# Linear attention: the small tokens' norms cut at TensorE's waits, their steps dealt at half tiles and queued behind the newest projection matmul

## The chip, the cores and the metric

The kernel runs on one core of one Trainium2 chip. The metric is device time in microseconds (us); the median of three runs stands for a kernel. The profile is one further execution, recorded instruction by instruction. Engines are named as in the profile: PE is TensorE (matmuls), DVE VectorE, ACT ScalarE, POOL GpSimd, SP the engine that issues most DMAs.

## The reference, cut to what matters

One inference step of a decoder of two layers, for 1024 prompt tokens plus 16 meta tokens and for 8 single tokens of running sequences. The first layer is gated linear attention (GLA), the second differential attention over a paged cache; each is followed by a squared-ReLU MLP, and each of the four steps by a residual and a layer norm:

```python
x = layer_norm(ALPHA * x + gla(x), g, b)
x = layer_norm(ALPHA * x + (relu(x @ w1) ** 2) @ w2, g, b)
# the same with diff_attention in place of gla, in layer 1
```

The 8 sample tokens and the 16 meta tokens (24 of 32 columns) go through the same weights as the prompt. In the kernel they are the **small tokens**, and have a path of their own.

## The kernel before

All work is in fp32. A prompt matmul is split in three (`mm3`, L205 to L208): high part by high part, high by low, low by high. Weights are loaded as raw pieces (L191), split on ACT (`whi`, L193) and POOL (`wlo`, L194).

**The GLA phase** takes the first 500 us or so. Head by head (four heads), `proj(h)` (L369) projects q and k (four tiles of 512 columns, 24 matmuls each) and v (four tiles of two halves, 24 matmuls of 256 columns in each half). After each tile it yields. Then, twice per head, `decays` (L429) works out the decay factors and the masked scores on DVE, ACT and small matmuls (L452, L467, L487), and `advance` (L492) steps the state through four blocks (L500 to L504), which is a chain from PE to DVE and back. When the heads are done, four r units follow (L843 on): eight steps of two projection tiles, each with a Silu (L855) and transposes (L859). Then the output projection begins (`w_out`), and beside it the decode of the sample tokens with their paged keys (L911, L942, L943).

**The small tokens** are a generator, `small_tokens` (L779). In order it does: the GLA output projection (`s_rows`, L702, two weight steps), residual and norm (`s_post`, L725, and `s_ln`, L744), the first MLP's w1 in two halves (`s_cols`, L715, four steps each, a ReLU, a square, four transposes at L790), w2 (eight steps), residual and norm, and the second layer's projection (`wd`: four steps for q and k, with the rotation, and two for v, here called wv, with the stores of the new k and v rows). A weight step loads 2 MB into both buffers of the pool `swt`, and yields; at the next call come its 16 matmuls (L712 in `s_rows`, L723 in `s_cols`) and the loads of the step after it. A norm has four transposes (L734), and two small matmuls with a matrix of 1/1024 (L748, L754) that give mean and variance across partitions; between them DVE works, and behind them ACT's logarithm and exponential (L758, L759) and DVE again. All of this was one piece, written together with the last weight step before it.

**How it is dealt.** `deal` (L819) runs the generator to its next yield. It is called once ahead of the loop, after every second tile of `proj(1)` to `proj(3)` (four per head), after the decays (both halves in head 1, the second half in heads 2 and 3), and once in each of the eight r steps: 25 calls. The generator had 25 pieces.

**What sets the order.** The framework orders each engine's queue when the program is built. By a timing model of its own it gives an engine, at each moment, that one of its ready instructions that was written earliest. So an instruction may run far behind its place in the program, when its data are late, and later-written work runs ahead of it. Once built, each engine's order is fixed: if the data come later than the model thought, the engine stands. `tc.issue_after(x)` makes the instructions written in its block that run on x's engine come behind x in that order; it costs no wait on the chip. DMAs issued from SP are one such queue.

Of the kernel before, what the change touches and what calls it, by code (L numbers as in the profile page):

```python
# [21 lines left out]
P = 128  # L22
D = 1024
T = 1024
NB = 8
# [89 lines left out]
def hybrid_step(ctx, tc, A, dbg=None, upto=9):  # L115
# [89 lines left out]
    def mm3(ps, ah, al, bh, bl, first, last):  # L205
        TE.matmul(ps, ah, bh, start=first, stop=False)  # L206
        TE.matmul(ps, ah, bl, start=False, stop=False)  # L207
        return TE.matmul(ps, al, bh, start=False, stop=last)  # L208


    p1 = ExitStack()
# [131 lines left out]
    ps = smt()  # L343
# [16 lines left out]
    ps = smt()  # L360
# [9 lines left out]
    def proj(h):  # L370
        hi, lo = qku if h == 0 else qk_unit(h)
        hv, lv = (w.rearrange("p (i k n) -> p i k n", i=2, n=P) for w in (hi, lo))
        for c in range(h == 0, 2):
            cs = slice(512 * c, 512 * c + 512)
            for i in range(2):
                ps = mmt()
                for k in range(NB):
                    mm3(ps, hv[:, i, k, :], lv[:, i, k, :], XH[:, k, cs], XL[:, k, cs], k == 0, k == NB - 1)
                evict_qk(c, i, ps)
                yield  # L380
        hi, lo = v0u if h == 0 else kunit(wi, 1024 + h * 256)
        hv, lv = (w.rearrange("p (k n) -> p k n", n=256) for w in (hi, lo))
        for c in range(2):
            for i2 in range(2):
                ps = mmt()
                for i in range(2):
                    t = 4 * c + 2 * i2 + i
                    for k in range(NB):
                        a = slice(t * P, (t + 1) * P)
                        mm3(ps[:, i * 256 : (i + 1) * 256], XH[:, k, a], XL[:, k, a], hv[:, k, :], lv[:, k, :], k == 0, k == NB - 1)  # L390
                S.copy(Yh[:, h, 4 * c + 2 * i2 : 4 * c + 2 * i2 + 2, :].rearrange("p i e -> p (i e)"), ps)
                yield


    def rstd_of(ssum, n, scale, pool):
# [126 lines left out]
    first = proj(0)  # L522
    parts = []

    def early(c):
# [173 lines left out]
        TE.transpose(ps[:, m * P : (m + 1) * P], so[:, m * P : (m + 1) * P], ident)  # L699
    V.tensor_copy(soT.rearrange("p (h m) t -> p m h t", m=2), ps[:, :256].rearrange("p (m h t) -> p m h t", m=2, h=GH))  # L700

    def s_rows(lhs, w, nk):  # L702

        ps = smt()
        for k in range(0, nk, 4):
            ts = [sload2(w, k), sload2(w, k + 2)]
            yield
            for j in (1, 0):
                for i in range(2):
                    for c in range(2):  # L710
                        o = (2 * i + c) * TS
                        TE.matmul(ps[o : o + TS, :], lhs[:, k + 2 * j + i, :], ts[j][:, i, c * 512 : (c + 1) * 512], start=k == 0 and j == 1, stop=k == nk - 4 and j == 0)  # L712
        return ps

    def s_cols(lhs, w, c0):  # L715

        ps = smt()
        for k in range(0, NB, 2):
            ts = [sload(w[x * P : (x + 1) * P, c0 : c0 + 2048]) for x in (k, k + 1)]
            yield  # L720
            for j in (1, 0):
                for c in range(4):
                    TE.matmul(ps[c * TS : (c + 1) * TS, :], lhs[:, k + j, :], ts[j][:, c * 512 : (c + 1) * 512], start=k == 0 and j == 1, stop=k == NB - 2 and j == 0)  # L723
        return ps

    def s_post(ps, ln, pool):

        sev = ps
        if pool is spool:
            sev = s2()  # L730
            S.copy(sev, ps)
        pt = smt()
        for j in range(4):
            TE.transpose(pt[:, j * P : (j + 1) * P], sev[:, j * P : (j + 1) * P], ident)  # L734

        pv = pt.rearrange("p (j q c t) -> p q c j t", j=4, q=2, c=2)
        z = pool.tile([P, NB, TS], F32, name="sz")
        for c in range(2):
            zc = z[:, 4 * c : 4 * c + 4, :]
            V.scalar_tensor_tensor(zc, sx[:, 4 * c : 4 * c + 4, :], ALPHA, pv[:, 0, c], ALU.mult, ALU.add)  # L740
            V.tensor_tensor(zc, zc, pv[:, 1, c], op=ALU.add)
        s_ln(z, ln, pool)

    def s_ln(z, ln, pool):  # L744
        s1 = pool.tile([P, TS], F32, name="ss1")
        V.tensor_reduce(s1, z.rearrange("p k t -> p t k"), op=ALU.add, axis=AX.X)
        pm = smt()
        TE.matmul(pm[:, :TS], inv, s1, start=True, stop=True)  # L748
# [3 lines left out]
        V.tensor_reduce(s1, z2.rearrange("p k t -> p t k"), op=ALU.add, axis=AX.X)  # L752
        pm = smt()
        TE.matmul(pm[:, :TS], inv, s1, start=True, stop=True)  # L754
# [3 lines left out]
        S.activation(y, v, AF.Ln)  # L758
# [19 lines left out]

    def small_tokens():  # L779

        s_post((yield from s_rows(soT, A["gla_w_out"][0], NB)), 0, spool)
        shT = s4().rearrange("p (k t) -> p k t", t=TS)
        for half in range(2):
            ps = yield from s_cols(sx, A["mlp_w1"][0], half * 2048)
            r = s2()
            S.activation(r, ps, AF.Relu)
            V.tensor_tensor(r, r, r, op=ALU.mult)
            pt = smt()
# [4 lines left out]
        s_post((yield from s_rows(shT, A["mlp_w2"][0], 32)), 1, spool)  # L793

        pa = yield from s_cols(sx, wd, 0)
# [4 lines left out]
        pb = yield from s_rows(sx, wd[:, 2048:3072], NB)  # L800
        svv = s2()
        S.copy(svv[64:, :], pb[64:, :])
        S.copy(svv[:64, :], svv[64:, :])
        V.tensor_tensor(svv[:64, :], svv[:64, :], pb[:64, :], op=ALU.add)
        for c in range(2):
            hs = slice(4 * c, 4 * c + 4)
            o = 64 + c * TS
            f = lambda ap: ap.rearrange("t h d -> t (h d)")
            dma(f(A["k_rows_p"][0, 0, 0:NM, hs, :]), sqkr[o : o + NM, :])
            dma(f(A["k_rows_s"][0, :, 0, hs, :]), sqkr[o + NM : o + NM + NS, :])  # L810
            dma(f(A["v_rows_p"][0, 0, 0:NM, hs, :]), svv[c * TS : c * TS + NM, :])
# [30 lines left out]
    for h in range(GH):  # L842
# [3 lines left out]
        for c in range(2):  # L846
            cs = slice(512 * c, 512 * c + 512)
            sil, pts = [], []
            for m in range(2):
                ps = mmt()  # L850
                for k in range(NB):
                    ms = slice(m * P, (m + 1) * P)
                    mm3(ps, hv[:, k, ms], lv[:, k, ms], XH[:, k, cs], XL[:, k, cs], k == 0, k == NB - 1)
                s_ = silt[:, m, c, :]
                act = S.activation(s_, ps, AF.Silu).ins  # L855
                sil.append(s_)
# [658 lines left out]
    def samples():  # L1515

        sev = s2()
        dma(sev, A["srow"])
        s_post(sev, 2, hp)
        yield  # L1520

    stats = ln_stats(hp)
# [25 lines left out]
    def samples_out():  # L1548
# [7 lines left out]
        for u in range(2):  # L1556
# [7 lines left out]
        s_ln(z, 3, hp)  # L1564
        for u in range(2):
            ps = smt()
            for j in range(4):
# [210 lines left out]
```

## Time and profile before

| | us |
|---|---|
| runs shown | 2803.95, 2810.49, 2811.46 |
| median | 2810.49 |
| the profiled execution | 2806.01 |
| its span in the profile | 2804.1 |
| TensorE busy in the span | 2722.0 |
| VectorE busy in the span | 1956.1 |

The profiled execution is 1.9 us longer than its span. "Busy" of TensorE is modelled from the matmuls' sizes; where it stands still, the profile names what ended the wait. A row of waits reads: engine, tile and line that waited, what it waited for, us in total, how often, the longest. A row of the timeline reads: start, duration, engine, line, operation, output<-inputs, shape, count, and in brackets the idle time before it with its releaser. A row of windows has the stretch, its length, the busy time of PE, of PE's weight loads, of DVE, ACT and POOL (with instruction counts), then the granted TensorE clock as a share of full speed, the share of the DMA engines in use, and GB/s.

### The profile page before, as it was taken

The page shows a single profiled execution, that of the slowest core. Times are in us where ns is not written, and L with a number is a line of the kernel's source. Part 1 is how long each engine was busy: PE and PEld are TensorE (multiplying, and loading weights), DVE is VectorE, ACT ScalarE, POOL GpSimd, SP SyncE. Part 2 cuts the span into 40 slices and gives each one's busy share as a digit, 9 for nine tenths or more (in the row PEclk, how much of TensorE's full clock was granted, in tenths as well). Part 3 has the DMA queues.
Part 4 walks back from the last instruction along what each step waited for, and adds up shares of the span by engine and source line. Part 5 has one row for each costly group of instructions (what it writes and reads, how often), then busy time and mean ns, then how long its engine had stood idle before and what let it go on. Part 6 is the DMA issues. An engine that isn't in the chain of part 4 may idle for free.

```text
span 2804.1 us, 52239 instructions
## 1 busy us (share of the span) xinstructions
PE 2722.0 (97%) x19849; PEld 2235.8 (80%) x19849; DVE 1956.1 (70%) x3011; ACT 1107.8 (40%) x2266; POOL 1096.6 (39%) x744
## 2 busy tenths in 40 slices
PE   9989999999999999999999999899999999999997
PEld 6867767987777777777798988777899889798985
DVE  5375453678877777777568730887648888978788
ACT  4334463152231221222242112777525546355553
POOL 2132112234343443434234222100026677686774
PEclk9999999999999999999999999999999999999998
DMA  7475544735889898888658995212144555555684
GB/s 240 161 243 213 198 162 175 268 96 178 310 315 335 304 348 303 322 313 315 241 182 315 357 372 167 58 57 77 36 121 91 102 146 113 139 124 114 133 187 99
DMA packets 275624, 562.81 MB, mean 201 GB/s; under 512 B 23510, under 2 KB 144412, under 8 KB 271276
## 3 DMA queue, kind: packets, MB, share of 16 engines
q1 hardware_dynamic: 256076, 522.75, 54.1%
q0 software_dynamic: 19296, 36.71, 8.1%
q8 instruction: 156, 2.56, 0.4%
q14 instruction: 96, 0.79, 0.1%
HBM read 533.00 MB, written 29.52 MB: 201 GB/s over the span
## 4 chain that ended last, share of the span: by engine, by line
PE 81%; DVE 9%; ACT 4%; DMA 3%; issue 2%; POOL 1%; SPq 0%; DVEq 0%; POOLq 0%; ACTq 0%
PE mmt L206 19%; PE mmt L207 18%; PE mmt L208 18%; PE smt L983 4%; PE axt L206 3%; PE axt L207 3%; PE axt L208 3%; PE smt L1354 2%; ACT as L1332 1%; PE prt L1328 1%; DVE pg L942 1%; DMA swt<-in_mlp_w 1%; PE axt L1349 1%; DVE XH L203 1%; PE smt L723 1%
## 5 line engine op out<-in xcount | busy, mean ns | idle before, releaser
L194 POOL TENSOR_TENSOR wlo<-raw,whi 128x512 fp32r<-128x512 f32 x252 | 358.4, 1435 | 708.7 <-ACT whi L193 584.9
L206 PE MATMUL mmt<-whi,XH 128*128 128x256 f32 (+1 forms) x1760 | 523.5, 300 | 1.1 <-DVE ast L1330 0.9
L207 PE MATMUL mmt<-wlo,XH 128*128 128x256 f32 (+1 forms) x1760 | 521.6, 298 | 0.4 <-POOL wlo L194 0.4
L206 PE MATMUL mmt<-XH,whi 128*128 128x512 f32 (+1 forms) x1216 | 435.5, 359 | 6.4 <-DVE Y L1053 3.0
L208 PE MATMUL mmt<-XH,wlo 128*128 128x512 f32 (+1 forms) x1216 | 431.9, 356 | 0.0
L208 PE MATMUL mmt<-whi,XL 128*128 128x256 f32 x1536 | 431.6, 284 | 0.1
L193 ACT CAST whi<-raw 128x512 fp32r<-128x512 f32 x252 | 150.3, 619 | 575.0 <-PE mmt L208 193.0
L206 PEld LDWEIGHTS mmt<-whi,XH 128*128 128x128 f32 x1760 | 330.0, 188 | 39.9 <-issue 26.1
L943 DVE TENSOR_REDUCE sc<-pg 128x16 f32<-128x1024 f32 x256 | 308.3, 1211 | 67.5 <-POOL pg L942 65.0
L207 PEld LDWEIGHTS mmt<-wlo,XH 128*128 128x128 f32 x1760 | 331.7, 188 | 15.8 <-issue 5.5
L942 DVE TENSOR_TENSOR pg<-pg,qb 128x1024 f32<-128x1024 f32 x192 | 265.7, 1391 | 63.7 <-DMA pg<-in_cache_k 57.1
L207 PE MATMUL mmt<-XL,whi 128*128 128x512 f32 x768 | 306.9, 400 | 0.0
L208 PEld LDWEIGHTS mmt<-whi,XL 128*128 128x128 f32 x1536 | 287.8, 188 | 7.3 <-issue 6.8
L206 PEld LDWEIGHTS mmt<-XH,whi 128*128 128x128 f32 x1216 | 229.3, 189 | 50.3 <-issue 7.6
L942 POOL TENSOR_TENSOR pg<-pg,qb 128x1024 f32<-128x1024 f32 x64 | 165.5, 2587 | 257.1 <-DMA pg<-in_cache_k 139.9
L208 PEld LDWEIGHTS mmt<-XH,wlo 128*128 128x128 f32 x1216 | 229.4, 189 | 35.7 <-issue 2.9
L206 PE MATMUL mmt<-whi,HH 128*128 128x512 f32 x512 | 205.4, 402 | 5.2 <-DVE Y L1167 3.5
L208 PE MATMUL mmt<-whi,HL 128*128 128x512 f32 x512 | 204.5, 399 | 0.0
L207 PE MATMUL mmt<-wlo,HH 128*128 128x512 f32 x512 | 204.0, 398 | 0.0
L1617 POOL TENSOR_TENSOR wlo<-RW,whi 128x512 fp32r<-128x512 f32 x96 | 165.8, 1766 | 61.1 <-ACT whi L1616 57.2
L1617 POOL TENSOR_TENSOR wlo<-rw,whi 128x512 fp32r<-128x512 f32 x92 | 156.9, 1774 | 81.7 <-ACT whi L1616 78.5
L207 PEld LDWEIGHTS mmt<-XL,whi 128*128 128x128 f32 x768 | 145.4, 189 | 39.3 <-issue 8.0
(438 smaller groups left out, 5720.3 us busy)
## 6 DMA issues: line engine op xcount, KB each, us to landing
pg<-in_cache_k SPq DMA_DIRECT2D x256, 512.0 KB
pg<-in_cache_v SPq DMA_DIRECT2D x256, 512.0 KB
raw<-in_mlp_w SPq DMA_DIRECT2D x164, 256.0 KB
swt<-in_mlp_w SPq DMA_DIRECT2D x32, 1024.0 KB
rw<-in_mlp_w SPq DMA_DIRECT2D x116, 256.0 KB
RW<-in_mlp_w POOLq DMA_DIRECT2D x96, 256.0 KB, 5.7
swt<-in_gla_w_in SPq DMA_DIRECT2D x12, 1024.0 KB
swt<-in_diff_w_in SPq DMA_DIRECT2D x12, 1024.0 KB
```

The costliest lines, as they stand in the source:

```text
L193: S.copy(hi[:, c], raw)
L194: G.tensor_tensor(lo[:, c], raw, hi[:, c].bitcast(F32), op=ALU.subtract)
L203: return eng.tensor_tensor(lo, src, hi.bitcast(F32), op=ALU.subtract)
L206: TE.matmul(ps, ah, bh, start=first, stop=False)
L207: TE.matmul(ps, ah, bl, start=False, stop=False)
L208: return TE.matmul(ps, al, bh, start=False, stop=last)
L723: TE.matmul(ps[c * TS : (c + 1) * TS, :], lhs[:, k + j, :], ts[j][:, c * 512 : (c + 1) * 512], start=k == 0 and j == 1, stop=k == NB - 2 a ...
L942: eng.tensor_tensor(pg, pg, qb, op=ALU.mult)
L943: return V.tensor_reduce(sc[:, n, :], pg.rearrange("p (h d) -> p h d", d=64), op=ALU.add, axis=AX.X).ins
L983: m = TE.matmul(acc[i * TS : i * TS + 16, :256], w[r, n, :], pg[r, i * 256 : (i + 1) * 256], start=n == 0, stop=n == NPG).ins
L1354: TE.matmul(out, at, v, start=j == 0, stop=j == t + 1)
L1617: G.tensor_tensor(lo[:, k, :], t, hi[:, k, :].bitcast(F32), op=ALU.subtract)
```

## The change

1. **The norm is cut.** `s_post` yields after the copy that precedes its transposes (only in the GLA phase), `s_ln` before each of its two mean matmuls. The MLP's halves yield before their transposes. These yields give 1: the next step waits for another engine. The weight steps' yields give 0. The generator now has 33 pieces: three more for each of two norms, one more for each of two halves.
2. **First loads earlier.** The first loads of a weight matrix (`rows_in`, `cols_in`) are written before the norm or ReLU that precedes its matmuls, not behind it.
3. **Calls at half tiles.** `proj` also yields in the middle of each tile (0; after a whole tile it yields 1), and the r steps have three further calls: in the middle of both tiles, and after the first. These calls, and those after even tiles, run a piece only if the last piece ended with a 1. The 25 calls of before run always.
4. **Queued behind.** `mm3` notes its last matmul in `newest`, and `deal` runs the generator in `tc.issue_after(newest[0])`: a piece's matmuls come behind the projection matmul written last before them.
5. In the later phases, where `s_post` and `s_ln` are used again, their yields are run through at once.

```diff
     def mm3(ps, ah, al, bh, bl, first, last):
...
-        return TE.matmul(ps, al, bh, start=False, stop=last)
+        r = TE.matmul(ps, al, bh, start=False, stop=last)
+        newest[0] = r.ins
+        return r
...
                     mm3(ps, hv[:, i, k, :], lv[:, i, k, :], XH[:, k, cs], XL[:, k, cs], k == 0, k == NB - 1)
+                    if k == 3:
+                        yield 0
                 evict_qk(c, i, ps)
-                yield
+                yield 1
...
+                    if i == 0:
+                        yield 0
...
-    def s_rows(lhs, w, nk):
+    def s_rows(lhs, w, nk, ts):
         ps = smt()
         for k in range(0, nk, 4):
-            ts = [sload2(w, k), sload2(w, k + 2)]
-            yield
+            if k:
+                ts = rows_in(w, k)
+            yield 0
...
             S.copy(sev, ps)
+            yield 1
         pt = smt()
...
-        s_ln(z, ln, pool)
+        yield from s_ln(z, ln, pool)
...
         V.tensor_reduce(s1, z.rearrange("p k t -> p t k"), op=ALU.add, axis=AX.X)
+        yield 1
         pm = smt()
...
         V.tensor_reduce(s1, z2.rearrange("p k t -> p t k"), op=ALU.add, axis=AX.X)
+        yield 1
         pm = smt()
...
-    def deal():
-        next(small, None)
+    chain = [0]
+
+    def deal(any_=True):
+        if any_ or chain[0]:
+            with tc.issue_after(newest[0]):
+                chain[0] = next(small, 0)
...
-        for n, _ in enumerate(proj(h)):
+        n = 0
+        for whole in proj(h):
+            if not whole:
+                deal(False)
+                continue
             if n == 1:
                 state_out()
             next(updates, None)
-            if n % 2:
-                deal()
+            deal(n % 2)
+            n += 1
...
                     mm3(ps, hv[:, k, ms], lv[:, k, ms], XH[:, k, cs], XL[:, k, cs], k == 0, k == NB - 1)
+                    if k == 3:
+                        deal(False)
+                if not m:
+                    deal(False)
```

More of the change, by code (lines that the diff above doesn't have):

```diff
@@ L520, in head_end @@
         G.tensor_tensor(Yh[:, h], Yh[:, h], bc(rr, [P, 8, 256], 2), op=ALU.mult)
-    first = proj(0)
+    first = (x for x in proj(0) if x)
     parts = []
@@ L713, in s_rows, with s_cols @@
         return ps
[L715 removed]
+    def s_cols(lhs, w, c0, ts):
         ps = smt()
         for k in range(0, NB, 2):
[L719 to L720 removed]
+            if k:
+                ts = cols_in(w, c0, k)
+            yield 0
             for j in (1, 0):
@@ L779, in small_tokens @@
     def small_tokens():
-        s_post((yield from s_rows(soT, A["gla_w_out"][0], NB)), 0, spool)
+        w1, w2 = A["mlp_w1"][0], A["mlp_w2"][0]
+        wo = A["gla_w_out"][0]
+        ps = yield from s_rows(soT, wo, NB, rows_in(wo, 0))
+        ts = cols_in(w1, 0, 0)
+        yield from s_post(ps, 0, spool)
         shT = s4().rearrange("p (k t) -> p k t", t=TS)
         for half in range(2):
-            ps = yield from s_cols(sx, A["mlp_w1"][0], half * 2048)
+            ps = yield from s_cols(sx, w1, half * 2048, ts)
+            ts = rows_in(w2, 0) if half else cols_in(w1, 2048, 0)
             r = s2()
@@ L792, in small_tokens @@
                           pt.rearrange("p (j c t) -> p c j t", j=4, c=4))
-        s_post((yield from s_rows(shT, A["mlp_w2"][0], 32)), 1, spool)
-        pa = yield from s_cols(sx, wd, 0)
+        ps = yield from s_rows(shT, w2, 32, ts)
+        ts = cols_in(wd, 0, 0)
+        yield from s_post(ps, 1, spool)
+        pa = yield from s_cols(sx, wd, 0, ts)
+        wv = wd[:, 2048:3072]
+        ts = rows_in(wv, 0)
         sqkr = s2()
@@ L1518, in samples @@
         dma(sev, A["srow"])
-        s_post(sev, 2, hp)
+        for _ in s_post(sev, 2, hp):
+            pass
         yield
@@ L1563, in samples_out @@
             V.scalar_tensor_tensor(zc, sx[:, 4 * u : 4 * u + 4, :], ALPHA, zc, ALU.mult, ALU.add)
-        s_ln(z, 3, hp)
+        for _ in s_ln(z, 3, hp):
+            pass
         for u in range(2):
```

10 lines of the change are left out of this document (8 added, 2 removed).

## The prediction, as put on record

> **What bounds the kernel now.** I read the page first, then the waits of TensorE over the stretch in which the small tokens' work is dealt out (150 to 515 us), then that stretch's timeline.
>
> ```profile
> span 2804.1 us, 52239 instructions
> PE 2722.0 (97%) x19849; PEld 2235.8 (80%) x19849; DVE 1956.1 (70%) x3011; ACT 1107.8 (40%) x2266; POOL 1096.6 (39%) x744
> ```
>
> ```profile
> PE smt L748 <- DVE ss L746: 3.5, 1, 3.5
> PE smt L723 <- DMA swt<-in_mlp_w: 2.7, 2, 2.2
> PE axt L452 <- DVE gAd L461: 2.7, 2, 1.6
> PE smt L712 <- DMA swt<-in_mlp_w: 2.2, 1, 2.2
> PE axt L501 <- DVE gS L504: 2.1, 2, 1.5
> PE smt L712 <- DMA swt<-in_gla_w_out: 1.3, 1, 1.3
> PE axt L500 <- ACT At L475: 1.2, 1, 1.2
> ```
>
> TensorE is the bound. It is busy in 97% of the span, so a wait matters only where TensorE itself stands. In these 365 us the rows add up to 15.7 us of standing still; those of the small tokens (L748, L723, L712) are 9.7 us. After the longest, TensorE also ran slowly:
>
> ```profile
> 185.00:190.00 5.00, 1.54 (x33) 1.30 (x28) 4.93 (x11) 0.42 (x2) 2.77 (x2) 0.74 0.98 325
> 190.00:195.00 5.00, 5.00 (x14) 3.91 (x15) 5.00 (x12) 2.03 (x6) 0.46 (x1) 0.57 0.59 172
> 235.00:240.00 5.00, 5.00 (x78) 3.74 (x71) 0.60 (x2) 1.77 (x5) 0.00 (x0) 0.66 0.71 234
> ```
>
> ```profile
> 166.83 0.59 ACT L391 COPY Y<-mmt 128x512 f32<-128x512 f32 x1 [5.09 <-PE mmt L208]
> ```
>
> ```profile
> 177.95 0.60 PE L734 MATMUL smt<-c_ident,s 128*128 128x128 f32 x4
> 189.01 0.64 PE L748 MATMUL smt<-ss,c_inv 128*128 128x32 f32 x2 [3.46 <-DVE ss L746]
> 189.83 0.80 PE L206 MATMUL mmt<-XH,whi 128*128 128x512 f32 x1
> 194.26 0.40 PE L207 MATMUL mmt<-XL,whi 128*128 128x512 f32 x1
> 195.20 0.40 PE L208 MATMUL mmt<-XH,wlo 128*128 128x512 f32 x1
> 210.45 1.92 PE L723 MATMUL smt<-swt,sx 128*32 128x512 f32 x16
> 234.14 2.64 PE L723 MATMUL smt<-swt,sx 128*32 128x512 f32 x16 [2.20 <-DMA swt<-in_mlp_w]
> ```
>
> The granted clock (third figure from the end) was 0.57 from 190 to 195. Ten projection matmuls took 4.43 us (189.83 to 194.26), where four took 0.94 us just after (194.26 to 195.20), that is 2.35 us for ten: 2.1 us lost on top of the 3.46. The piece at 234.14 took 2.64 us where the one at 210.45 took 1.92.
>
> **The first norm and the first half of the MLP: nothing, 0 us.** Each piece is now to be queued behind the newest projection matmul written before it, and the norm is cut at its waits. The order edge binds only where a piece stands ahead of that matmul in TensorE's order. It does not here. The first norm's steps are dealt between the halves of head 1's v tiles. The last of those tiles was evicted at 166.83, while the norm's transposes stand at 177.95, its first mean matmul at 189.01, the next weight pair at 210.45. They run late because they wait for the decode state and for 2 MB of weights per piece, not because of where they are written. So every edge is already met, and among ready instructions all of these still rank ahead of head 2's work. L748 was put where the builder's own timing expected the sum of L746, and VectorE came 3.46 us later than that. The change alters neither, so I leave this wait and its slow spell in place. Bounds: if a shifted priority removes it, -5.6 us; if an order moves against it, +2 us, the size of the other waits.
>
> **One call lost.** Before, 25 pieces met 25 calls. After, there are 33 pieces, and 25 calls that always run; the others run only when the last piece ended at a wait. All such extra steps find a conditional call next, except one: the second half of the first MLP ends its ReLU in the last call of head 2's projections, and the next call is the whole one inside head 2's second decay. It is spent on four transposes. From there each weight pair comes one whole call later, and the last pair (wv, second four rows) is left for the loop behind the r projections. Where that moves something:
>
> ```profile
> 339.12 1.06 PE L712 MATMUL smt<-swt,s 128*32 128x512 f32 x8
> 347.36 0.50 PE L206 MATMUL mmt<-XH,whi 128*128 128x512 f32 x1
> 389.59 1.92 PE L712 MATMUL smt<-swt,s 128*32 128x512 f32 x16
> 407.49 0.41 PE L754 MATMUL smt<-ss,c_inv 128*128 128x32 f32 x2
> 411.06 0.70 PE L500 MATMUL axt<-Y,At 128*128 128x256 f32 x2 [1.20 <-ACT At L475]
> 416.45 1.92 PE L723 MATMUL smt<-swt,sx 128*32 128x512 f32 x16
> 418.30 0.70 PE L501 MATMUL axt<-gS,t 128*128 128x256 f32 x2
> 431.51 1.92 PE L723 MATMUL smt<-swt,sx 128*32 128x512 f32 x16
> 488.19 1.92 PE L712 MATMUL smt<-swt,sx 128*32 128x512 f32 x16
> ```
>
> ```profile
> 408.38 1.28 ACT L758 ACT_TABLE_LOAD   x1
> 409.81 1.20 ACT L475 COPY At<-gAd 32x128 f32<-32x128 f32 x4
> 423.76 1.58 ACT L855 ACTIVATE st<-mmt 128x512 f32<-128x512 f32 x3
> ```
>
> Up to 339 the later call is still met. The fourth pair of w2 (339.12) may now only follow head 3's last v tile, so about 347; those behind it follow at the pace of the loads, 12 us apiece (210.45 to 234.14 are two), and the eighth (389.59) goes to about 400, behind the second r unit's first two tiles. TensorE has projection tiles for all of that time: 0 us. Its norm then moves too: L754 may come only in the tile that starts after the Silu at 423.76, so about 427.
>
> This takes work out of the one place of the stretch where TensorE has nothing else: until 424 the chain of head 3's last decay and state steps sets the time. Three things leave it: the table load and logarithm ahead of the At copies, worth the 1.20 us that TensorE waits at 411.06; the pair at 416.45, after which L501 starts at 418.30 (1.85 us); L754's 0.41. One thing enters: the eighth w2 pair, up to 1.92 us, of which I take 1. Sum -2.4 us, bounds -3.5 and +1.
>
> A page has another price here. The Trainium skill (ScalarE: Activation LUTs, "What ACT_TABLE_LOAD costs") gives about 2.66 us for each change of table, 1.28 of load and 1.38 of drain; by it the gain would be 1.4 us larger. This trace shows no drain: the load at 408.38 lasts 1.28 us and the copies start at 409.81, one 0.23 us activation later.
>
> **The tail.** From 431.51 to 488.19 five pairs stand behind five r units. Five still do, but the last pair follows them, in the output projection. The pair that used the idle place at 416 now lies where TensorE is full: +1.9 us. Its weights can only be asked for when the pair at 488 is done. Waits for swt were 0.5 to 2.2 us in this trace; I take 1.5, bounds 0 and 3 (2.20 and the 0.72 us that 234.14 was slow).
>
> ```profile
> 495.80 1.97 SPq L811 DMA_DIRECT2D out_v_rows_p<-s  x1
> 499.41 2.65 SPq L191 DMA_DIRECT2D raw<-in_gla_w_out  x2
> 505.89 4.13 SPq L911 DMA_DIRECT2D pg<-in_cache_k  x4
> ```
>
> ```profile
> 508.65 0.62 ACT L193 CAST whi<-raw 128x512 fp32r<-128x512 f32 x1 [13.23 <-DMA raw<-in_gla_w_out]
> ```
>
> ```profile
> 600.00:650.00 50.00, 47.62 (x213) 37.90 (x213) 37.37 (x40) 19.90 (x36) 17.18 (x10) 1.00 0.39 117
> 650.00:700.00 50.00, 49.09 (x210) 39.02 (x209) 45.49 (x44) 9.79 (x17) 19.14 (x10) 1.00 0.61 196
> 700.00:750.00 50.00, 47.67 (x278) 35.59 (x277) 38.33 (x43) 13.83 (x25) 18.71 (x11) 1.00 0.78 277
> ```
>
> Behind it come the stores of v rows (495.80), and in the same SP queue raw weights and the first key pages. These may come 10 to 15 us later. The pages are dealt as background work, which TensorE's own matmuls cover; a late start costs only where VectorE is tight, 600 to 750, where TensorE stands 5.6 us in all: 0 taken, bounds -3 and +3.
>
> **Sum.** 0 + 0 - 2.4 + 1.9 + 1.5 + 0 = +1.0 us. The profiled execution took 2806.0 us, so 2807.0 on its scale. The runs shown are 2803.95, 2810.49 and 2811.46, and with the profiled one their mean is 2808.0; its median lies 4.5 above the profile. On that middle I forecast 2809. About 0.3%, 8.4 us from the median, is what a measurement of this kernel can tell from no change.
>
> **Rivals.**
> *The waits go.* If the builder's new order puts the small pieces later than their data, L748's 3.46 and 2.1 go, and the swt waits (1.3, 2.7, 2.2) with two slow spells of about 0.7: 5.6 + 6.2 + 1.4 = 13.2. The rest of the sum stays: 2808.0 + 1.0 - 13.2 = 2796. For it: 9.7 us of small-token waits exist and nothing else need use them. Against: no edge binds before 339. Chance 0.27. The Trainium skill (TensorE: Matmul & The Clock Gate, Part 1) lets the clock halve after an idle window of about 3.4 us; by it the 2.2 us gaps would cost nothing more, and this rival would give 1.4 us less. The trace disagrees: 0.66 was granted from 235 to 240, after a gap of 2.20.
>
> *Slower: the last pair blocks SP's queue.* SP issues in order. If the stores of the last pair stand ahead of the raw weights of the second output unit and come 10 to 12 us late, the cast at 508.65 (which already waited 13.23 us for such a raw) comes at about 520, past the 513 or so at which TensorE has used the first unit on both halves of the tokens (estimated: from 490.1, 192 matmuls of 256 columns at half the 0.235 us of one of 512). That is 7 us, a slow spell of 2, and the 3 us wait of the pair itself: 12 us, 2820. It decides from a delay of about 5 us on. For it: the two raws at 499.41 do stand behind those stores now. Against: the order is made anew, and the raws then come first if they are ready first. Chance 0.20.
>
> **Numbers.** Forecast 0.53 (own range 2803 to 2819: all its bounds, without the -5.6 that is the first rival's), waits go 0.27, SP blocked 0.20. Range 2793 to 2820, reaching into both rivals. Faster by over 0.3% 0.27, same 0.53, slower 0.20.
>
> **What would show it.** Right: L748 still waits about 3 us near 189; the w2 pairs keep their places before 339, then lie 8 us or more later; no Ln between head 3's At copies; a pair of wv after 490. Wrong: L748 and the swt rows gone from TensorE's waits (first rival), or new waits of L206 on whi or wlo between 505 and 530 (second). A change of over 5 us that arises after 750 would mean that I missed a place altogether.

## The result, and the profile after

The changed kernel takes 2819.31 us (median of 20 runs, 2811.05 to 2838.1), the kernel before in the same session 2809.28 (20 runs, 2799.43 to 2815.79): a ratio of 1.0037 with an interval of 1.0026 to 1.0048, so 10 us slower. Its profiled execution took 2819.02 us (before 2806.0).

```profile
span 2817.1 us, 52238 instructions
PE 2724.5 (97%) x19849; PEld 2236.5 (79%) x19849; DVE 1957.5 (69%) x3011; ACT 1109.5 (39%) x2267; POOL 1089.9 (39%) x744
```

The engines are as busy as before (TensorE 2724.5 against 2722.0), so the 13 us of span are not work. The waits of TensorE from 150 to 530 us, in the same view that the prediction began with:

```profile
PE smt L768 <- DVE ss L765: 3.6, 1, 3.6
PE axt L460 <- DVE gAd L469: 2.6, 2, 1.6
PE axt L460 <- issue: 2.5, 1, 2.5
PE smt L729 <- DMA swt<-in_gla_w_out: 2.1, 1, 2.1
PE axt L508 <- ACT At L483: 1.8, 1, 1.8
PE smt L741 <- DMA swt<-in_mlp_w: 1.7, 2, 1.3
PE smt L729 <- DMA swt<-in_mlp_w: 1.1, 1, 1.1
```

Lines are shifted by the diff: L748 is now L768, L712 L729, L723 L741, L452 L460. The longest wait stays (3.6 us, before 3.5), and so do those for weights: 2.1, 1.7 and 1.1 us, against 1.3, 2.7 and 2.2. What is new here is 2.5 us at L460 that no releaser explains.

To see where the time went I use three marks that each trace has: the first matmul of the output projection (call it P), the projection matmul near 706 us that waits 1.25 us for HL in every kernel (M), and the end of the span. Two rows of before and two of after, from the timeline of TensorE:

```profile
490.05 0.38 PE L206 MATMUL mmt<-whi,XH 128*128 128x256 f32 x1
706.03 0.50 PE L206 MATMUL mmt<-XH,whi 128*128 128x512 f32 x1 [1.25 <-DVE HL L203]
```

```profile
486.57 0.39 PE L206 MATMUL mmt<-whi,XH 128*128 128x256 f32 x1
708.95 0.50 PE L206 MATMUL mmt<-XH,whi 128*128 128x512 f32 x1 [1.24 <-DVE HL L203]
```

P comes 3.5 us earlier than before; from P to M it takes 222.4 us instead of 216.0, so 6.4 more; from M to the end 2108.2 instead of 2098.1. The table in the next section shows that only the middle one of these three differences lasts from profile to profile.

Most of that difference arises in the output projection itself. Its end is marked by the first matmul of 512 columns behind it, before and after:

```profile
584.05 0.48 PE L206 MATMUL mmt<-XH,whi 128*128 128x512 f32 x1
```

```profile
585.27 0.39 PE L206 MATMUL mmt<-XH,whi 128*128 128x512 f32 x1
```

From P to here it takes 94.0 us before and 98.7 after, so 4.7 more; from here to M 122.0 and 123.7, so 1.7 more.

Inside P to M, the last pair and the waits that are new with it (timeline of TensorE of the changed kernel):

```profile
484.71 1.92 PE L729 MATMUL smt<-swt,sx 128*32 128x512 f32 x16
496.33 1.92 PE L729 MATMUL smt<-swt,sx 128*32 128x512 f32 x16
537.40 0.50 PE L206 MATMUL mmt<-whi,XH 128*128 128x256 f32 x2 [0.96 <-ACT whi L193]
538.78 0.38 PE L207 MATMUL mmt<-wlo,XH 128*128 128x256 f32 x1 [0.17 <-POOL wlo L194]
540.66 0.39 PE L207 MATMUL mmt<-wlo,XH 128*128 128x256 f32 x1 [0.20 <-POOL wlo L194]
554.01 0.38 PE L207 MATMUL mmt<-wlo,XH 128*128 128x256 f32 x1 [0.37 <-POOL wlo L194]
642.27 0.50 PE L206 MATMUL mmt<-whi,HH 128*128 128x512 f32 x1 [2.24 <-DVE Y L1208]
657.80 0.50 PE L206 MATMUL mmt<-whi,HH 128*128 128x512 f32 x1 [1.22 <-DVE Y L1208]
661.80 0.50 PE L206 MATMUL mmt<-whi,HH 128*128 128x512 f32 x1 [0.92 <-DVE Y L1208]
```

The next to last pair is at 484.71. The last, whose 2 MB go into the same two buffers, follows at 496.33, within the output projection, without a wait of its own. Then TensorE waits four times for converted weights and three times for VectorE. Before, these are all its waits from 500 to 698, and none is for weights:

```profile
628.01 0.50 PE L206 MATMUL mmt<-XH,whi 128*128 128x512 f32 x1 [0.68 <-DVE HL L203]
641.36 0.50 PE L206 MATMUL mmt<-whi,HH 128*128 128x512 f32 x1 [1.70 <-DVE HL L203]
658.87 0.51 PE L206 MATMUL mmt<-whi,HH 128*128 128x512 f32 x1 [0.38 <-DVE Y L1167]
```

What SP and ScalarE did about 530, first before, then after:

```profile
529.35 0.90 SPq L191 DMA_DIRECT2D raw<-in_gla_w_out  x2
```

```profile
533.13 0.62 ACT L193 CAST whi<-raw 128x512 fp32r<-128x512 f32 x1 [7.55 <-DMA raw<-in_gla_w_out]
534.22 0.62 ACT L193 CAST whi<-raw 128x512 fp32r<-128x512 f32 x1 [0.47 <-DMA raw<-in_gla_w_out]
```

```profile
509.48 0.33 SPq L841 DMA_DIRECT2D out_v_rows_p<-s  x1
513.70 0.36 SPq L952 DMA_DIRECT2D pg<-in_cache_k  x1
515.82 13.87 SPq L952 DMA_DIRECT2D pg<-in_cache_k  x12
529.79 0.39 SPq L191 DMA_DIRECT2D raw<-in_gla_w_out  x1
531.44 0.39 SPq L191 DMA_DIRECT2D raw<-in_gla_w_out  x1
```

```profile
536.73 0.62 ACT L193 CAST whi<-raw 128x512 fp32r<-128x512 f32 x1 [12.57 <-DMA raw<-in_gla_w_out]
538.62 0.62 ACT L193 CAST whi<-raw 128x512 fp32r<-128x512 f32 x1 [1.27 <-DMA raw<-in_gla_w_out]
```

The first page is asked for 27.1 us behind P (513.70 - 486.57), before 15.8. Twelve more follow in one row up to 529.7, and behind them the third unit's raw weights: asked for at 529.79 and 531.44 (43.2 and 44.9 us behind P; before, 39.3 and 39.8), cast 6.9 and 7.2 us later (before, the first 3.8). As many pages stand ahead of them in SP's queue as before (13 and 14; before 14), so it is not a changed place in that queue that makes them late. VectorE, which multiplies the pages, has less to do meanwhile. The window from 490 to 520 of before, then of after (busy time of DVE is the third busy time):

```profile
490.00:520.00 30.00, 30.00 (x257) 29.95 (x254) 14.95 (x26) 4.40 (x8) 5.87 (x4) 1.00 0.99 344
```

```profile
490.00:520.00 30.00, 30.00 (x255) 28.42 (x254) 9.69 (x23) 2.65 (x5) 2.57 (x2) 1.00 0.91 286
```

The DMA engines move less as well, 286 GB/s instead of 344. From 20 to 30 us behind P, where SP's queue stands at the stores of the v rows, their share is 0.64; before it is 1.03 (a packet counts where it starts, so a share can pass 1).

### The profile page after: what moved, and what is told of

It reads as the page before. It is cut to its first block, busy times and chain, and to the rows that moved or that the text cites. A ratio compares the mean times of both kernels' runs of the same rounds, so it can differ in the third digit from the quotient of the medians.

```text
span 2817.1 us, 52238 instructions
## 1 busy us (share of the span) xinstructions
PE 2724.5 (97%) x19849; PEld 2236.5 (79%) x19849; DVE 1957.5 (69%) x3011; ACT 1109.5 (39%) x2267; POOL 1089.9 (39%) x744
## 4 chain that ended last, share of the span: by engine, by line
PE 75%; DVE 11%; DMA 5%; ACT 4%; issue 3%; POOL 2%; SPq 1%; DVEq 0%; POOLq 0%; ACTq 0%
PE mmt L206 17%; PE mmt L207 17%; PE mmt L208 17%; PE smt L1024 4%; PE axt L206 3%; PE axt L207 3%; PE axt L208 3%; PE smt L1395 2%; ACT as L1373 1%; DVE pg L983 1%; DVE XH L203 1%; DVE Y L1733 1%; DVE RX L1634 1%; PE prt L1369 1%; DMA swt<-in_mlp_w 1%
## 5 line engine op out<-in xcount | busy, mean ns | idle before, releaser
L206 PEld LDWEIGHTS mmt<-XH,whi 128*128 128x128 f32 x1216 | 229.5, 189 | 49.4 <-issue 8.4
```

## Experiments

My theory after the first profile: the lost call puts the last pair behind P, and pages and weights of the output projection come late by it. The rivals: the cuts, the half tiles or the queueing cost by themselves; or the loss lies behind M (+10 us in the first profile), where the orders of the engines differ in a few places only.

All runs in one table. "Page" is the first page's issue less P; "output projection" runs from P to the first matmul of 512 columns behind it. The last column is the ratio to the kernel before, timed on the same chip, with its interval.

| kernel | P | page | output projection | P to M | M to end | ratio |
|---|---|---|---|---|---|---|
| before | 490.1 | 15.8 | 94.0 | 216.0 | 2098.1 | |
| d_queue_only | 486.7 | 15.9 | 93.9 | 214.5 | 2104.0 | 0.9996 (0.9982 to 1.0010) |
| h_no_relu_cut | 491.7 | 17.8 | 93.9 | 215.8 | 2103.7 | 0.9983 (0.9970 to 0.9995) |
| changed | 486.6 | 27.1 | 98.7 | 222.4 | 2108.2 | 1.0037 (1.0026 to 1.0048) |
| a_again | 490.0 | 27.0 | 99.4 | 220.7 | 2104.7 | 1.0038 (1.0024 to 1.0052) |
| e_no_queue | 490.2 | 26.8 | 99.0 | 222.4 | 2094.4 | 1.0042 (1.0027 to 1.0057) |
| c_one_call_less | 489.4 | 27.1 | 99.0 | 220.9 | 2099.0 | 1.0024 (1.0010 to 1.0038) |
| b_call_back | 497.9 | 16.3 | 95.0 | 217.7 | 2102.7 | 1.0008 (0.9994 to 1.0022) |
| i_two_calls_less | 487.9 | 40.4 | 102.4 | 235.0 | 2101.7 | 1.0035 (1.0017 to 1.0053) |
| j_pages_held | 488.2 | 28.4 | 93.5 | 223.8 | 2104.9 | 1.0025 (1.0013 to 1.0036) |
| g_v_rows_queue | 490.0 | 25.6 | 99.2 | 221.3 | 2095.1 | 1.0018 (1.0004 to 1.0032) |
| k_y_late | 491.6 | 20.4 | 99.4 | 220.8 | 2099.7 | 1.0015 (0.9997 to 1.0033) |
| l_before_y_late | 490.9 | 12.6 | 95.8 | 219.4 | 2099.6 | 1.0021 (1.0007 to 1.0036) |
| n_last_unloaded | 485.3 | 16.3 | 94.5 | 216.7 | 2100.9 | 1.0005 (0.9992 to 1.0017) |
| q_1mb_more | 493.2 | 18.5 | 94.8 | 217.4 | 2104.3 | 1.0018 (1.0003 to 1.0032) |
| m_2mb_more | 492.0 | 20.6 | 100.0 | 231.9 | 2101.9 | 1.0061 (1.0039 to 1.0082) |

The first three have one and the same order on every engine, so their spread is that of the measurement: 5 us in P, 0.1 in the output projection, 1.5 in P to M, 6 in M to end, and 0.17% in the ratio. The interval of h_no_relu_cut misses 1 although its order is that of before. So a ratio within 0.2% of 1 shows nothing here by itself, even where its interval misses 1.

**a_again**: the changed kernel, unchanged.

> The changed kernel once more, unchanged, for a second profile. Lost call (my step: the last wv pair falls behind the r units): ratio 1.003 to 1.005, and the places where it lies behind the kernel before are the same as in the first profile: +3 to +4 us by 700. Chance in the late stretches: the jumps at 1910, 2333 and 2450 (about +9 us together in the first profile, where the order on every engine is that of the kernel before) are gone or elsewhere. A cause that lasts: they are there again.

P to M is 220.7, and the output projection takes 99.4; from M to the end it takes 2104.7, about what d_queue_only and h_no_relu_cut take. The 10 us behind M in the first profile were scatter, and the rival that puts the loss there falls.

**d_queue_only**: the kernel before with point 4 of the change alone.

```diff
...
-        next(small, None)
+        with tc.issue_after(newest[0]):
+            next(small, None)
```

> The kernel before with its pieces queued behind the newest projection matmul, and neither the cut norm nor the half tiles. My step that no edge binds: ratio 0.999 to 1.001, and the profile of the kernel before, a measure also of how much two profiles of one order differ in the late stretches. If the edges bind: a ratio beyond 0.3% either way.

0.9996, and every engine's order is that of before. Queueing alone does nothing.

**c_one_call_less**: the kernel before with one deal fewer.

```diff
-            if c or h == 1:
+            if h == 1 or (c and h == 3):
                 deal()
```

> The kernel before with one deal fewer (none at head 2's second decay), nothing else of the change: its last pieces slip by one call as they do in the changed kernel. Lost call: ratio 1.002 to 1.005 over the kernel before. The cut norm, the half tiles or the queueing: 0.999 to 1.001.

1.0024, and P to M is 220.9, the output projection 99.0, like those of the changed kernel. A lost call alone brings the loss in P to M.

**b_call_back**: the changed kernel with the call given back.

```diff
             with tc.issue_after(newest[0]):
                 chain[0] = next(small, 0)
+                if any_ and chain[0]:
+                    chain[0] = next(small, 0)
```

> The change with its lost call given back: a call that always runs and finds a step of the chain pending runs that step and the next piece, so that the last wv pair stands inside the r units again. Lost call: the loss goes, ratio 0.998 to 1.001, and the waits of L206 and L207 on whi and wlo between 537 and 554 are gone. The cut norm, the half tiles or the queueing themselves: ratio stays at 1.003 to 1.004.

1.0008, not told from 1; page as before, output projection 95.0, and P to M 2.3 above the mean of the first three rows. One wait for wlo of 0.8 us is left at 558, so that part of the expectation did not hold fully. Its profile lost 8 us ahead of P, 3 of them before 100 us.

**h_no_relu_cut**: the changed kernel without one line.

```diff
             V.tensor_tensor(r, r, r, op=ALU.mult)
-            yield 1
             pt = smt()
```

> The changed kernel without its one yield behind the ReLU of the first MLP's halves; all other cuts, the half tiles and the queueing stay. Its instructions then stand in the order of the kernel before on every engine. Lost call: ratio 0.999 to 1.001, and the output projection takes 94 us from its first matmul to the first of 512 columns behind it, as before. If the other cuts cost something by themselves: a ratio above 1.001.

0.9983. With the yield behind the ReLU gone, the order of all five engines is the order before: the cut norms, the earlier first loads, the half tiles and the queueing together move no instruction. Without this one yield the change has no effect, neither gain nor loss.

**e_no_queue**: the changed kernel without the queueing.

```diff
-            with tc.issue_after(newest[0]):
-                chain[0] = next(small, 0)
+            chain[0] = next(small, 0)
```

> The changed kernel without the queueing behind the newest projection matmul; the cuts, the half tiles and the lost call stay. Crowded DMA behind the lost call: nothing comes back, ratio 1.002 to 1.004, first page about 27 us behind the start of the output projection, waits for whi and wlo of 1.5 to 2.5 us. If the queueing, harmless in the kernel before, costs together with the cuts: ratio 0.999 to 1.001.

1.0042, pages at 26.8, output projection 99.0, six waits for whi and wlo of 1.8 us in all: nothing comes back. The queueing takes no part in the loss. It does in what the change wins ahead of P: from the Exp behind head 3's last decays to P it takes 83.0 us here, 81.4 in both profiles of the changed kernel, and 83.7 in all three of the order before. Here the second norm's second small matmul (L775) stands at 411.93, within that stretch; in the changed kernel it comes at 424.10.

**i_two_calls_less**: two deals fewer.

```diff
-            if c or h == 1:
+            if h == 1:
                 deal()
```

> The kernel before with two deals fewer (none at the second decay of heads 2 and 3): two wv pairs lie in the output projection. Lost call: twice the cost or more in the output projection, 94 us become 103 to 105, ratio 1.004 to 1.008. If one lost call costs by its place in head 2's decay and not by the tail: about as with one deal fewer, 1.002 to 1.003.

Two pairs lie behind P, the pages come 40.4 us behind it, and P to M takes 235.0, 19.6 more than the mean of the first three rows (215.4), 8.5 of them in the output projection. That is more than twice the 5.4 of one call. The ratio, 1.0035, is lower than that would give (about 1.007); its interval reaches to 1.0053.

**j_pages_held**: the kernel before, its pages held by their page table; no pair is moved and no more bytes. Two page steps are dealt at once when the table is let go.

```diff
-    dma(ptab, A["page_table"])
...
-                if side and (n == 4 if scaled else n < 12):
+                if side and not scaled and n == 2:
+                    with tc.issue_after(steps_v[-1]):
+                        V.memset(ptab, 0)
+                    dma(ptab, A["page_table"])
+                    for _ in range(2):
+                        next(side)
+                if side and (n == 4 if scaled else 1 < n < 12):
                     next(side)
```

> The kernel before with the page table, and so the first page, held until the third tile of the output projection is evicted (about 10 us later); all pairs stay where they are. Late pages: waits for whi and wlo of 1 to 3 us appear in the output projection, which takes 95.5 to 97 us instead of 94, ratio 1.0005 to 1.0015. The pair itself: 94 us, ratio 0.999 to 1.0005.

The ratio is 1.0025, more than I expected, and the loss is at another place: the output projection takes 93.5 us (before 94.0, the changed kernel 98.7), but TensorE then waits for VectorE, and from there to M it takes 130.2 us instead of 122.0. The rows of TensorE, then those of VectorE ahead of 633:

```profile
606.06 0.50 PE L206 MATMUL mmt<-XH,whi 128*128 128x512 f32 x1 [2.63 <-DVE HL L203]
633.37 0.79 PE L206 MATMUL mmt<-XH,whi 128*128 128x512 f32 x1 [3.87 <-DVE HL L203]
711.97 0.50 PE L206 MATMUL mmt<-XH,whi 128*128 128x512 f32 x1 [1.25 <-DVE HL L203]
```

```profile
626.88 2.31 DVE L941 TENSOR_TENSOR pg<-pg,qb 128x1024 f32<-128x1024 f32 x1
629.23 1.22 DVE L942 TENSOR_REDUCE sc<-pg 128x16 f32<-128x1024 f32 x1
630.37 2.35 DVE L1128 SCALAR_TENSOR_TENSOR Y<-Y,ht 128x1024 f32<-128x1024 f32 x2
632.63 1.28 DVE L203 TENSOR_TENSOR HL<-mmt,HH 128x512 fp32r<-128x512 f32 x2
```

So a late start of the pages costs by itself, nearly 9 us over the mean of the first three rows behind the output projection. VectorE was busy 10.84 us from 490 to 520 here and 14.95 before. 100 us later a page's product and sum (626.88 and 629.23) stand in its order ahead of the HL that TensorE waits for at 633.37.

**g_v_rows_queue**: the last pair's four stores issued by ScalarE.

```diff
...
-            dma(f(A["v_rows_p"][0, 0, 0:NM, hs, :]), svv[c * TS : c * TS + NM, :])
+            nc.scalar.dma_start(f(A["v_rows_p"][0, 0, 0:NM, hs, :]), svv[c * TS : c * TS + NM, :])
...
```

> The changed kernel with the four stores of the v rows issued from ScalarE's queue instead of SyncE's; nothing else moves by more than a place. Late pages (the last pair's stores hold SyncE's queue, the first pages come 8 us later and fill the DMA engines when the third unit's raw weights are asked for): the first page comes 2 to 8 us earlier, the waits for whi and wlo between 535 and 557 (1.7 to 2.5 us) go, the output projection takes 96 to 97 us instead of 98.7 to 99.5, ratio 1.002 to 1.003. The pair itself and its weights: 98.7 to 99.5 as in the changed kernel, waits stay, ratio 1.0035 to 1.004.

Inconclusive. The pages came at 25.6 instead of 27, the output projection takes 99.2 and P to M 221.3: the stores alone were not what held SP. The ratio, 1.0018, is below the changed kernel's 1.0037, but the two intervals overlap. In the changed kernel the first store waited 4.6 us for the loads of the residual x (Y) ahead of it; here the next load in the queue waited 3.5 us for raw weights in its place.

**k_y_late** and **l_before_y_late**: in the changed kernel and in the kernel before, two of the four 1 MB loads of Y are held until tiles 3 and 5 of the output projection.

```diff
+                if not scaled and n in (2, 4):
+                    u2 = 2 + (n == 4)
+                    with tc.issue_after(steps_v[-1]):
+                        V.memset(Yt[:, 0, u2 * 256 : u2 * 256 + 1], 0.0)
+                    y_in(u2)
...
```

> The changed kernel, its lost call kept, with the loads of the last two quarters of the residual x (Y, 1 MB each) held until tiles 3 and 5 of the output projection are evicted, so that they no longer stand ahead of the pages in SyncE's queue. Late pages: the first page comes 5 us earlier or more (22 us behind the start of the output projection instead of 27), VectorE is busier between 490 and 520 than the 8.6 to 9.7 us of the changed kernel, the stretch from 480 to 700 loses 1 to 4 us less than in the changed kernel (+4.6 to +7.4), ratio 1.001 to 1.003. The pair itself: stretch and ratio as in the changed kernel, 1.0035 to 1.004.

> The kernel before with the same two loads held. If each us by which the pages come earlier is worth half a us, as the held pages cost about half a us for each us later: first page 10 to 13 us behind the start of the output projection instead of 15.8, ratio 0.998 to 0.9995. If before was at the point where the pages are early enough: 0.9995 to 1.0005.

In the first the pages come at 20.4 instead of 27, but the output projection still takes 99.4 and P to M 220.8: the raw weights of the third unit are asked for at 536.0, behind a Y load and two more pages, and TensorE waits 2.3 us for them. In the second the pages come at 12.6, earlier than before, and P to M is 219.4, 4.0 above the mean of the first three rows, with a wait of 1.57 us for whi at 553. (The ratios, 1.0015 and 1.0021, are about as far from 1 as those of one order differ.) Half a us lost or won for each us of the pages, as I had put it, falls. What one of pages, raw weights and Y got earlier here, another got later.

**n_last_unloaded**: the changed kernel, the lost call kept, but the last pair multiplies with the weights of the pair before it, so that 2 MB are not loaded, and in each v row of the small tokens half of the sum is formed with the wrong rows of the weight.

```diff
...
-            if k:
+            if k and not same:
                 ts = rows_in(w, k)
...
-        pb = yield from s_rows(sx, wv, NB, ts)
+        pb = yield from s_rows(sx, wv, NB, ts, True)
```

> The changed kernel, its lost call kept, but the last wv pair loads no weights of its own and multiplies with those of the pair before it, so half of the small tokens' v rows is computed from the wrong rows of the weight; 2 MB less are moved, and the pair stands directly behind the fifth one, before the output projection. Crowded DMA or in-order SyncE: first page 16 us behind the start of the output projection or earlier, no waits for whi and wlo, the stretch from 480 to 700 us within 1.5 us of the kernel before, ratio 0.998 to 1.0005. If the loss lies in the decays or in the cuts themselves: ratio 1.002 to 1.004.

All of the loss is gone, within the spread: page at 16.3, output projection 94.5, P to M 216.7, ratio 1.0005. No wait for whi or wlo is left, and VectorE has more to do from 490 to 520 than in the changed kernel (17.76 us, there 9.69). Both last pairs stand ahead of P, so this run takes the bytes and the pair's own 1.9 us out of the output projection together; the next two runs add bytes alone.

```profile
490.00:520.00 30.00, 30.00 (x256) 30.00 (x255) 17.76 (x25) 0.53 (x2) 4.67 (x2) 1.00 0.98 355
```

**m_2mb_more** and **q_1mb_more**: the kernel before with a copy of 2 MB, or of 1, that nobody reads.

```diff
...
+        if u < 2:
+            with tc.issue_after(y.ins):
+                dma(A["extra"][u * 256 : (u + 1) * 256, :], A["diff_w_in"][0][u * 256 : (u + 1) * 256, 2048:3072])
```

> The kernel before with 2 MB more to move (a copy from DRAM to DRAM in two halves, whose result nobody reads), queued on SyncE behind the first two quarters of the residual x, at the start of the output projection. All pairs stay where they are. Crowded DMA (the lost call moves 2 MB of weights into the only stretch in which the DMA engines are full, and pages and raw weights come later by that): first page 5 us or more later than 15.8 us behind the start of the output projection, waits for whi and wlo appear, the stretch from 480 to 700 us grows by 3 to 6 us, ratio 1.001 to 1.0025. In-order SyncE alone (the last pair's stores wait there, the bytes do not matter): the stretch grows by less than 1.5 us, ratio 0.9985 to 1.0005.

> The kernel before with 1 MB more to move instead of 2 (the first half of that copy), in the same place of SyncE's queue. Crowded DMA: the stretch from 480 to 700 us grows by 4 to 9 us, between nothing and the 15.8 us of 2 MB, ratio 1.0015 to 1.004. If there is slack for the first MB, or if the cost of 2 MB was a single order that happened to be bad: less than 2 us, ratio 0.999 to 1.001.

With 2 MB the pages come at 20.6, the output projection takes 100.0 and P to M 231.9: 16.5 us more than the mean of the first three rows, nearly three times the upper end that I expected. 6.1 of them lie in the output projection, and 10.4 behind it, where the changed kernel lost little. The ratio is 1.0061. TensorE waits for whi and wlo, and then once for long:

```profile
544.92 0.51 PE L207 MATMUL mmt<-whi,XH 128*128 128x256 f32 x2 [1.80 <-ACT whi L194]
559.56 0.50 PE L207 MATMUL mmt<-whi,XH 128*128 128x256 f32 x2 [1.34 <-ACT whi L194]
643.41 0.80 PE L207 MATMUL mmt<-XH,whi 128*128 128x512 f32 x1 [7.80 <-DVE HL L204]
659.16 0.50 PE L207 MATMUL mmt<-whi,HH 128*128 128x512 f32 x1 [2.61 <-DVE Y L1168]
```

With 1 MB the output projection takes 94.8 and P to M 217.4, only 2.0 more, less than the 4 to 9 expected: in this profile there was slack for about the first MB. (The ratio, 1.0018, is above what 2 us give, 1.0007, which its interval still holds.) (The copy both reads and writes DRAM, so 2 MB of it are more than 2 MB of weights.)

## Why the prediction was wrong

I forecast "same", 2809; it is 2819. Step by step:

- **First norm and first half of the MLP, 0 us: right.** L768 waits 3.6 us, the first w1 pair is at 210.68 (before 210.45). That no edge binds there is shown by d_queue_only, and h_no_relu_cut shows more: none of the other cuts moves anything.
- **One call lost, through the ReLU's yield: right**; without that yield, in h_no_relu_cut, the change moves nothing. The order of the pieces is the one that I forecast, but the w2 pairs moved less: the fourth is at 341.25 (about 347 forecast), the eighth at 395.41 (about 400), 2 and 6 us later than before and not 8 or more. L775 is at 424.10 (427), no logarithm stands between head 3's At copies, and the last pair is behind P.
- **The gain of 2.4 us in the starved stretch: right, and kept up to P.** The Exp behind head 3's last decays and the last gS of its state, before and after (timelines of ScalarE and VectorE):

```profile
406.33 0.63 ACT L478 ACTIVATE t<-gb 128x512 f32<-128x512 f32 x1 [2.17 <-PE axt L452]
```

```profile
421.18 0.48 DVE L504 SCALAR_TENSOR_TENSOR gS<-gS,geb,axt 128x256 f32<-128x256 f32 x1 [1.22 <-PE axt L502]
```

```profile
405.19 0.63 ACT L486 ACTIVATE t<-gb 128x512 f32<-128x512 f32 x1 [1.39 <-PE axt L460]
```

```profile
417.51 0.48 DVE L512 SCALAR_TENSOR_TENSOR gS<-gS,geb,axt 128x256 f32<-128x256 f32 x1 [1.23 <-PE axt L510]
```

  It takes 12.3 us instead of 14.85, so 2.5 less. One of my three terms is wrong: the wait for At did not go, it is 1.8 instead of 1.2. From this Exp to P it takes 81.4 us in both profiles of the changed kernel and 83.7 in all three of the order before, so 2.3 are still won at P. P itself does not show it (486.6 and 490.0 against 490.1, 486.7 and 491.7), because what runs ahead of the Exp scatters by 5 us, and because TensorE has a new wait there that I did not foresee, at L460 (2.5 and 3.0 us in the two profiles, absent in the three of the order before).
- **The tail: the step that failed.** I took 1.9 for the pair, 1.5 for its wait and 0, bounds -3 and +3, for pages and raw weights, 3.4 in all. P to M grew by 7.0, 5.3 and 7.0 us over the mean of 215.4 (changed, a_again, e_no_queue). The pair's 1.9 came, and it waited for nothing. The 0 failed, and for the raw weights of the third unit, a place that I did not see. With one call lost (these three and c_one_call_less) the output projection takes 98.7 to 99.4 us instead of 93.9 to 94.0; less the pair that is 2.9 to 3.6 us, of which 1.7 to 2.5 are listed as waits for whi and wlo. The first of these weights is cast 49.4 to 50.2 us behind P, in the three profiles of the order before 41.0 to 44.0. The place that I did name, "only where VectorE is tight, 600 to 750", cost little: from the output projection's end to M the four profiles take 121.3 to 123.7 us against 120.6 to 122.0.
- **What makes those weights late** the runs do not settle fully. They point to the last pair's 2 MB more than to the start of the pages: pages 12.6 us later than before, without more bytes, leave the output projection at 93.5 (j_pages_held); pages 6.7 us earlier than in the changed kernel leave it at 99.4 (k_y_late); 2 MB added to the kernel before bring it to 100.0 (m_2mb_more), 1 MB only to 94.8 (q_1mb_more); and without the pair's 2 MB it is 94.5 (n_last_unloaded). But the copy of m_2mb_more is more traffic than the weights are, and n_last_unloaded moves the pair too. SP's standing at the stores may have a part: g_v_rows_queue and k_y_late raise the DMA share from 20 to 30 us behind P from 0.64 to 0.78 and 0.89, and win nothing in the output projection, but neither brings it to the 1.03 of before.
- **Late pages can cost behind the output projection**, as j_pages_held shows. Why the changed kernel, whose pages come nearly as late (27.1 us behind P, there 28.4), loses so little there, no run shows.
- **The slow rival named the right queue, with a wrong carrier.** It gave 2820 by way of the second unit's raw weights, between 505 and 530. Those were cast at 495.53 already, earlier than before (508.65), and the pair's wait of 3 us did not come either. That its 2820 lies next to the 2819 measured is luck. The stores alone do not carry the loss: g_v_rows_queue takes them out of SP's queue, and the output projection stays at 99.2.
- **The waits go: wrong.** L768's 3.6 us and the waits for swt are still there, as the first view of the changed kernel shows.
- **The signs that I had named did not test the tail.** L768 still waits, no logarithm stands between the At copies and a pair of wv comes after 490, as I had put down for "right"; they follow from the lost call, and say nothing of what it costs. The new waits on whi and wlo came 7 to 24 us behind the window of 505 to 530 that I had named for the slow rival.
- **"A change of over 5 us after 750 would mean that I missed a place"**: the first profile showed that, and a_again (2104.7 from M to the end) and e_no_queue (2094.4) take it back.

Left open: P to M explains 6.4 us (the mean of three profiles). With 2.3 won ahead of P, and 2.5 to 3.0 lost at L460 if that wait counts in full, this makes about 7 us, and the medians say 10 (7.3 to 13.5). The rest is in no place that lasts from profile to profile.

No version was found that beats the kernel before; the changed kernel without the ReLU's yield is that kernel.

## What to carry to other kernels

When work is dealt out by a count of calls, look for the piece that falls off the end, and price what it takes along: its bytes, and what queues behind them, before its matmuls. Find the stretch in which the DMA engines are full, and ask of each change whether it brings bytes into it; here 1 MB more cost 2.0 us and 2 MB 16.5, in one profile each. Take two or three profiles of one order before you believe a difference that appears far from the edit, and compare stretches between two instructions rather than times since the start: in the three profiles of the order before, P scatters by 5 us and the 84 us ahead of it by less than 0.1.

## What the runs showed that was not expected

- **Twice the bytes cost eight times as much.** 1 MB more in a stretch with a DMA share near 1 cost 2.0 us from P to M, 2 MB cost 16.5. It is one profile each, and most of the 16.5 hangs on the one wait of 7.80 us, so it is no law.
- **One order, three profiles.** before, d_queue_only and h_no_relu_cut execute the same instructions in the same order on each engine, and reach P at 490.1, 486.7 and 491.7 us.
- **TensorE stood for 1.6 to 3.0 us ahead of the last of 64 small matmuls of 32 columns in a row** (L460, parts of the masked scores) in every kernel with the ReLU's yield and in none without it, where such a row has 32 there. The trace has no releaser. A row of 160 in the kernel before (405.79) runs without such a stop, so the count alone isn't it; nothing tried here tells why.
- **A wait can cost more than its length.** In i_two_calls_less TensorE waits 3.10 us at 553.56, and the granted clock (third figure from the end) is 0.53 from 555 to 560. In j_pages_held it waits 3.87 us at 633.37, and the clock is 0.61 from 635 to 640. After 2.24 us at 642.27 in the changed kernel it stays at 1.00. The three rows:

```profile
555.00:560.00 5.00, 5.00 (x26) 5.00 (x26) 4.84 (x5) 0.00 (x0) 1.28 (x1) 0.53 0.79 265
```

```profile
635.00:640.00 5.00, 5.00 (x16) 3.90 (x15) 3.67 (x3) 0.77 (x2) 3.77 (x2) 0.61 0.17 61
```

```profile
640.00:645.00 5.00, 2.76 (x13) 2.24 (x13) 3.01 (x4) 1.03 (x2) 2.82 (x3) 1.00 0.47 121
```

The Trainium skill (TensorE: Matmul & The Clock Gate, Part 1) lets the clock fall after an idle window of about 3.4 us, and says that this window runs freely. The waits of 3.87 and 2.24 us agree with that, the one of 3.10 is a little short of it, and the fall to 0.66 after 2.20 us at 234, which the prediction shows, does not agree.
